# A hybrid attention block on one core: the indexer's keys projected in its queries' loop, first weights as two half loads, selection rounds spread, a gate moved ahead of the sparse values

## The chip, the cores and the metric

The kernel runs on one core of one Trainium2 chip. The metric is device time in microseconds (us), the median of several executions. Before the change it is 780.78 us, the median of three (780.55, 780.78, 782.25). The engines are TensorE (PE, matmuls; PEld is its weight load), VectorE (DVE), ScalarE (ACT), GpSimd (POOL) and SyncE (SP), which here only issues DMAs. Each runs its own list of instructions in a fixed order and waits at semaphores for the others.

## What is computed

One block of an encoder over 512 positions and 1024 channels, in float32:

```python
proj = x @ w_in[layer]
q_a, k_a, v_a, q_i, k_i, w_i, q_s, k_s, v_s, g_a, g_b = jnp.split(proj, IN_OFFSETS, axis=-1)
y_a = dsa_sequence(...)     # sparse attention
y_s = sb_sequence(...)      # stick-breaking attention
merged = sigmoid(g_a + b) * (y_a @ w_branch_dsa) + sigmoid(g_b + b) * (y_s @ w_branch_sb)
x = layer_norm(ALPHA * x + merged @ w_out, ...)
u, g = jnp.split(x @ w_ffn_in, 2, axis=-1)
h = gelu(causal_dwconv(u, conv_w, conv_b)) * g
x = layer_norm(ALPHA * x + h @ w_ffn_out, ...)
```

The sparse branch chooses its keys with an "indexer": from queries q_i (8 heads of 64), one shared set of keys k_i (64 wide) and 8 weights w_i per position it computes a score per pair, the sum over heads of w_i * relu(q_i . k_i), and keeps the 128 best keys of each query. Then it is ordinary attention over those, with a relative bias, 8 heads. The stick-breaking branch has 8 heads too; its weights are products of sigmoids along the keys, which a running product (a scan) gives.

## The kernel before

**Numbers.** A float32 matrix is used as a sum of a rounded high half and a low half (`whi`/`wlo`, `xh`/`xl`). Each product is three matmuls: high by high, high by low, low by high. ScalarE makes the high half (L94, L261), VectorE or, for the weights named in `POOL_LO`, GpSimd the low half by a subtraction (L96, L262).

**Weights.** `Stream` (L52) holds the list `order` of all weight pieces, up to 512 KB each. A `get` loads three pieces ahead (L85) into raw buffers and splits three ahead (L86) into a ring of three pairs `whi`, `wlo`. There are three raw buffers (`rawp`, L128); before the change the eight pieces of the indexer's query weights have other raw buffers, the four tiles of tag "q" (L245). All loads are issued by SP, and up to the 13th piece an explicit order holds them in the order of the program (L66).

**PSUM.** Two pools of four banks each, `psA` and `psB` (`pa` and `pb` in the code). A tile takes a bank until all that reads it is done.

**Who orders the work.** The program is written as one list. A planner then simulates it with its own costs and gives each engine its order: of the instructions that are ready and have a buffer, it takes the one that stands first in the program. `tc.issue_after` adds an order on one engine by hand.

**Start (L175 to L280).** Nine matmuls on zeros (`WARM`) run first. Then a loop over the eight chunks k of 128 channels loads and splits the chunk of x and the chunk `qi{k}` of the indexer's query weights and adds 12 matmuls of 384 columns to the four banks `qps` (queries 128 to 511; the first 128 need no selection). In the first two rounds of the loop, four steps (`next(values)`) of the stick-breaking values are done too, with half pieces `vs00` and `vs01`; their four sums are in `psB`.

**Indexer (L313 to L376).** `idx_queries` (L313) empties the four `qps` banks into the halves `qi`. Behind 12 matmuls of filling, `idx_keys` (L324) projects keys and weights w_i (24 matmuls of 512 columns, 72 rows out) and empties them. Then two small matmuls build the bias line (L551). `idx_scores` computes 24 dots (three query blocks j, eight heads; two matmuls each in a `psA` bank), each with a relu on ScalarE (L353) and an accumulation on VectorE (L358). `select` (L360) takes 16 rounds for each block j: a round finds the 8 largest of a row (L367) and replaces them (L368), so 48 rounds in all. `select_some(n)` puts n of them at that place of the program. 16 stand between the dots, and the others behind the scans of the first seven stick-breaking heads, by `ROUNDS = 3, 3, 4, 5, 5, 6, 6`.

**Filling.** The list `FILL` (L32) names the projections that TensorE does between the parts of the heads, in order: `vs`, `qs`, `ks` are the stick-breaking values, queries and keys, `va`, `qa`, `ka` the sparse ones, `gb`, `ga` the gates, `bs` the branch's output. `fill(n)` (L528) emits steps of three matmuls until n are out. `proj_t` (L196) makes one 128-row block in a `psA` bank; `proj_v` (L208) makes values in four banks at once, over eight chunks. They are emptied by ScalarE and VectorE (L231 and L232 for values, L305 and L306 for queries, L295 to L297 for keys, ScalarE alone for gates).

**Heads (L576 to L593).** Sixteen heads in turn, eight stick-breaking, eight sparse. In each: the next head's logits, `fill(15)`, transposes of this head's weights (L389), the next head's scans on VectorE (L445), the rounds, `fill(15)`, the weighing (L405), `fill(15)`. The first sparse head needs all selections done (L569).

**Behind the heads.** The merge, the output projection, the first norm. Each block of 128 positions is normed on VectorE (L656 last) and transposed on TensorE by `turn` (L699), whose result is split by ScalarE (L707) and VectorE (L708) into `x1h`, `x1l`. The feed-forward part (L719) takes its first three pieces in two halves of the positions, `t_lo` for all three, then `turn` for the last block, then `t_hi` for all three. The rest is not touched.

Of the kernel before, what the change touches and what calls it, by code (L numbers as in the profile page):

```python
# [31 lines left out]
FILL = ("vs qs0 ks0 qs1 ks1 qs2 ks2 gb0 gb1 qs3 ks3 gb2 gb3 qa0 ka0 gb4 qa1 ka1 va gb5 bs0 bs1 qa2 ka2 gb6 gb7 bs2 bs3 "  # L32
        "qa3 ka3 ga0 ga1 ga2 ga3 ga4 ga5").split()
GAP = 15
ROUNDS = 3, 3, 4, 5, 5, 6, 6
# [16 lines left out]
class Stream:  # L52


    def __init__(self, tc, raw, ring, pieces, ahead_load, ahead_split, place=None, lo_on_pool=()):
        self.tc, self.nc, self.raw, self.ring, self.pieces, self.last = tc, tc.nc, raw, ring, pieces, None
        self.place = {} if place is None else place
        self.raw_place = {}
# [22 lines left out]

    def _advance(self, upto):
# [3 lines left out]
        while self.ns < min(n, upto + self.asp, self.nl):  # L86
# [7 lines left out]
            nc.scalar.activation(hi[:, :w], t[:, :w], AF.Copy)  # L94
# [14 lines left out]
def tile_block(ctx: ExitStack, tc: tile.TileContext, xT, xN, w_qi, w_ki, w_t, w_v, w_br, w_o, w_fi, w_fo,  # L109
# [33 lines left out]
    order = [(f"qi{k}", w_qi[k]) for k in range(KC)]  # L143
    for kk in (1, 0):
        order.insert(kk + 1, (f"vs0{kk}", w_v[0, 0][:, kk * 512:kk * 512 + 512]))
    order.append(("vs1", w_v[0, 1]))

    def pieces(t):
        if t == "ki":
            return [(t, w_ki)]  # L150
        if t in ("vs", "va"):
            return [(f"{t}{g}", w_v[int(t == "va"), g]) for g in range(2 * (t == "vs"), 4)]
# [4 lines left out]
    for t in ["ki"] + FILL:  # L157
# [13 lines left out]
    place = {}  # L171
# [24 lines left out]
    def proj_t(key, M=128, bank=pa):  # L196

        wh, wl = st.get(key)
        ps = bank(f"{key}_ps")
        for k in range(KC):  # L200
            c = slice(k * M, k * M + M)
            nc.tensor.matmul(ps[:M], wh[:, c], xh[k], start=(k == 0), stop=False)  # L202
            nc.tensor.matmul(ps[:M], wh[:, c], xl[k], start=False, stop=False)  # L203
            nc.tensor.matmul(ps[:M], wl[:, c], xh[k], start=False, stop=(k == KC - 1))  # L204
            yield 3
        return ps

    def proj_v(which, name):  # L208

        pss = [(pb if which == "vs" else pa)(f"{name}_ps{i}") for i in range(NB)]  # L210
        for g in range(4):
            halves = which == "vs" and g == 0
            if not halves:
                wh, wl = st.get(f"{which}{g}")
            for kk in range(2):
                k = 2 * g + kk
                c = slice(kk * 512, kk * 512 + 512)
                if halves:
                    wh, wl = st.get(f"{which}{g}{kk}")
                    c = slice(0, 512)  # L220
                for i in range(NB):
                    r = slice(i * 128, i * 128 + 128)
                    nc.tensor.matmul(pss[i], xh[k][:, r], wh[:, c], start=(k == 0), stop=False)
                    nc.tensor.matmul(pss[i], xh[k][:, r], wl[:, c], start=False, stop=False)
                    nc.tensor.matmul(pss[i], xl[k][:, r], wh[:, c], start=False, stop=(k == KC - 1))
                    yield 3
        vt = []
        for i in range(NB):
            v = bp.tile([128, H, 2, 64], F32R, tag="v", bufs=4, name=f"{name}{i}")
            src = pss[i].rearrange("p (h d) -> p h d", h=H)  # L230
            nc.scalar.activation(v[:, :, 0, :], src, AF.Copy)  # L231
            nc.vector.tensor_sub(v[:, :, 1, :], src, r32(v[:, :, 0, :]))  # L232
            vt.append(v)
# [688 lines left out]
```

## Time and profile before

| what | value |
|---|---|
| median of three executions | 780.78 us |
| the profiled execution's own time | 781.24 us |
| its span, first to last instruction | 779.5 us |
| TensorE busy | 767.4 us (98%) |
| VectorE busy | 473.9 us (61%) |
| ScalarE busy | 331.1 us (42%) |
| GpSimd busy | 117.6 us (15%) |
| moved by DMA | 84.01 MB |
| granted TensorE clock, mean | 0.999 |

How to read the lines: a time, a duration, the engine, the line of the kernel, the operation, the tiles written and read, the shapes, a count, and in brackets how long the engine had been idle and what ended it. Groups have count, busy time in us, mean ns of one, and idle time before. Matmuls are pipelined: the profile's duration of one reaches past the start of the next. TensorE's busy share hides short waits, so the distance from one start to the next is of more use.

### The profile page before, as it was taken

Reading aid. Unit: us, or ns where it says so; the run is one execution under the profiler, and the core shown is the slowest. Engines: PE = TensorE matmul, PEld = TensorE weight load, DVE = VectorE, ACT = ScalarE, POOL = GpSimd, SP = SyncE. Lnnn points to the kernel's source line nnn. Section 1 sums busy time; section 2 is a strip of 40 time slices with the busy share of each in tenths; the row PEclk is TensorE's granted clock in tenths of the full one; section 3 lists DMA queues with packets and bytes.
Section 4 is the critical chain, followed back from the end, with each engine's and each line's share of the span. In section 5 each row is a group of like instructions: output and inputs, shape, how many; then the busy total and the mean of one; then the engine's idle time right before and its main releaser. Section 6 shows DMA issues by size and latency. Waiting matters only on the chain.

```text
span 779.5 us, 9704 instructions
## 1 busy us (share of the span) xinstructions
PE 767.4 (98%) x3696; PEld 643.8 (83%) x3696; DVE 473.9 (61%) x782; ACT 331.1 (42%) x518; POOL 117.6 (15%) x123
## 2 busy tenths in 40 slices
PE   9999999999999999999999999999999999999996
PEld 7878888887788888888889888888888888888885
DVE  5579776899887665477744545435354543536345
ACT  5474665564555837745102433323323332332300
POOL 1012464446634210000001000000000000000002
PEclk9999999999999999999999999999999999999999
DMA  7445413222323232127502333222222222322302
GB/s 260 144 152 175 134 56 109 93 71 81 108 94 124 84 131 78 61 99 259 209 0 79 114 106 104 85 82 109 107 98 93 108 82 82 112 104 80 138 27 82
DMA packets 26591, 84.01 MB, mean 108 GB/s; under 512 B 3816, under 2 KB 4200, under 8 KB 26544
## 3 DMA queue, kind: packets, MB, share of 16 engines
q1 hardware_dynamic: 22320, 72.87, 26.2%
q10 hardware_dynamic: 2576, 6.29, 3.0%
q0 software_dynamic: 1648, 4.22, 1.6%
q8 instruction: 29, 0.48, 0.3%
q14 instruction: 18, 0.15, 0.1%
HBM read 77.06 MB, written 4.21 MB: 104 GB/s over the span
## 4 chain that ended last, share of the span: by engine, by line
PE 91%; DVE 7%; issue 1%; ACT 1%; POOL 1%; POOLq 0%; DVEq 0%; ACTq 0%
PE u_ps L724 5%; PE d_ps L752 5%; PE d_ps L753 5%; PE d_ps L754 5%; PE u_ps L725 5%; PE g_ps L724 5%; PE g_ps L723 5%; PE g_ps L725 5%; PE u_ps L723 5%; PE av_ps L405 2%; PE ga_ps L203 2%; PE ga_ps L202 2%; PE ga_ps L204 2%; PE o_ps L683 2%; PE o_ps L682 2%; PE o_ps L684 2%
## 5 line engine op out<-in xcount | busy, mean ns | idle before, releaser
L94 ACT ACTIVATE whi<-raw 128x1024 fp32r<-128x1024 f32 (+1 forms) x114 | 119.6, 1049 | 225.3 <-PE d_ps L754 84.9
L96 DVE TENSOR_TENSOR wlo<-raw,whi 128x1024 fp32r<-128x1024 f32 (+1 forms) x95 | 115.2, 1213 | 161.8 <-ACT whi L94 155.0
L723 PE MATMUL u_ps<-x1h,whi 128*128 128x512 f32 (+1 forms) x192 | 71.4, 372 | 0.2 <-ACT x1h L707 0.2
L724 PE MATMUL u_ps<-x1l,whi 128*128 128x512 f32 (+1 forms) x192 | 71.4, 372 | 0.1
L725 PE MATMUL u_ps<-x1h,wlo 128*128 128x512 f32 (+1 forms) x192 | 71.3, 371 | 0.0
L724 PE MATMUL g_ps<-x1l,whi 128*128 128x512 f32 (+1 forms) x184 | 69.9, 380 | 0.0
L723 PE MATMUL g_ps<-x1h,whi 128*128 128x512 f32 (+1 forms) x184 | 69.9, 380 | 0.0
L725 PE MATMUL g_ps<-x1h,wlo 128*128 128x512 f32 (+1 forms) x184 | 69.9, 380 | 0.0
L752 PE MATMUL d_ps<-whi,hh 128*128 128x512 f32 (+1 forms) x178 | 65.5, 368 | 0.0
L753 PE MATMUL d_ps<-wlo,hh 128*128 128x512 f32 (+1 forms) x178 | 65.4, 368 | 0.0
L754 PE MATMUL d_ps<-whi,hl 128*128 128x512 f32 (+1 forms) x178 | 61.4, 368 | 0.0
L96 POOL TENSOR_TENSOR wlo<-raw,whi 128x1024 fp32r<-128x1024 f32 x19 | 45.8, 2412 | 34.8 <-ACT whi L94 34.8
L731 POOL MEMSET u<- 128x2 f32 x22 | 2.2, 101 | 268.7 <-DVE c L736 260.8
L723 PEld LDWEIGHTS u_ps<-x1h,whi 128*128 128x128 f32 x192 | 36.2, 188 | 6.7 <-ACT x1h L707 0.5
L724 PEld LDWEIGHTS u_ps<-x1l,whi 128*128 128x128 f32 x192 | 36.2, 188 | 6.5 <-DVE x1l L708 0.3
L725 PEld LDWEIGHTS u_ps<-x1h,wlo 128*128 128x128 f32 x192 | 36.2, 188 | 6.3
L725 PEld LDWEIGHTS g_ps<-x1h,wlo 128*128 128x128 f32 x184 | 34.6, 188 | 6.6
L723 PEld LDWEIGHTS g_ps<-x1h,whi 128*128 128x128 f32 x184 | 34.6, 188 | 6.5
L724 PEld LDWEIGHTS g_ps<-x1l,whi 128*128 128x128 f32 x184 | 34.6, 188 | 6.4
L737 ACT ACTIVATE c<-c,cwt 128x512 f32<-128x512 f32 x22 | 15.9, 723 | 55.6 <-DVE c L736 55.6
L394 DVE TENSOR_TENSOR ptl<-tr_ps,pth 128x512 fp32r<-128x512 f32 (+1 forms) x48 | 27.9, 594 | 18.2 <-ACT pth L393 17.6
L753 PEld LDWEIGHTS d_ps<-wlo,hh 128*128 128x128 f32 x178 | 33.6, 189 | 5.6
(463 smaller groups left out, 1775.3 us busy)
## 6 DMA issues: line engine op xcount, KB each, us to landing
raw<-in_w_fi_dram SPq DMA_DIRECT2D x44, 512.0 KB, 3.2
raw<-in_w_t_dram SPq DMA_DIRECT2D x32, 512.0 KB, 3.3
raw<-in_w_fo_dram SPq DMA_DIRECT2D x22, 512.0 KB, 3.2
raw<-in_w_br_dram SPq DMA_DIRECT2D x8, 512.0 KB, 3.1
raw<-in_w_o_dram SPq DMA_DIRECT2D x8, 512.0 KB, 3.8
raw<-in_w_v_dram SPq DMA_DIRECT2D x7, 512.0 KB, 4.2
xr<-in_xT_dram SPq DMA_DIRECT2D x8, 256.0 KB, 4.8
raw_qi<-in_w_qi_dram SPq DMA_DIRECT2D x8, 256.0 KB, 4.9
```

The costliest lines, as they stand in the source:

```text
L94: nc.scalar.activation(hi[:, :w], t[:, :w], AF.Copy)
L96: eng.tensor_sub(lo[:, :w], t[:, :w], r32(hi[:, :w]))
L202: nc.tensor.matmul(ps[:M], wh[:, c], xh[k], start=(k == 0), stop=False)
L203: nc.tensor.matmul(ps[:M], wh[:, c], xl[k], start=False, stop=False)
L394: lows = nc.vector.tensor_sub(tl[:, :width], ps[:, :width], r32(th[:, :width]))
L723: nc.tensor.matmul(ps[:, c], wh[:, kc], x1h[:, k, c], start=(k == 0), stop=False)
L724: nc.tensor.matmul(ps[:, c], wh[:, kc], x1l[:, k, c], start=False, stop=False)
L725: nc.tensor.matmul(ps[:, c], wl[:, kc], x1h[:, k, c], start=False, stop=(k == KC - 1))
L737: nc.scalar.activation(c, c, AF.Gelu_apprx_tanh, bias=cwt[:, f, 3:4])
L752: nc.tensor.matmul(ps, hh[f][:, r], wh[:, c], start=start, stop=False)
L753: nc.tensor.matmul(ps, hh[f][:, r], wl[:, c], start=False, stop=False)
L754: nc.tensor.matmul(ps, hl[f][:, r], wh[:, c], start=False, stop=stop)
```

## The change

- **Keys in the queries' loop.** The indexer's key weights `ki` become the fourth piece of the stream and are split into two tiles of tag "q". From the second round of the loop on, the three key matmuls of the chunk follow the twelve of the queries (in the second round those of both chunks), in a bank of `psB`. `idx_keys` then only empties that bank. The bias line is built straight behind the loop.
- **Values.** The stick-breaking values are no longer begun in the loop. They start as the first filling, in the four `psA` banks, with whole pieces. In the last of the four pieces (g = 3) the steps of both kinds of values are sorted by block, so that one block is finished after the other.
- **Banks.** The dots and the transposed weights w_i use `psB`, not `psA`. The 12 matmuls of filling ahead of `idx_keys` go.
- **First weights.** `qi0` is loaded as two halves of 256 columns, `qi00` and `qi01`. The high half of the first is made by VectorE, those of all others by ScalarE as before; the first chunk's `xl` is ordered behind that copy. The query weights use the three raw buffers of `rawp` like all others.
- **Rounds.** `ROUNDS` goes. One round follows each scan, and `fill(15, 2)` places one more behind every second step of filling; two such fills a head make five rounds a head for the first seven.
- **FILL.** `gb5` stands before `va`, not behind it.
- **Feed-forward.** `turn` for the last block stands ahead of the third `t_lo` piece, not behind it.

The diff, without the functions that only move:

```diff
-FILL = ("vs ... qa1 ka1 va gb5 bs0 bs1 qa2 ka2 gb6 gb7 bs2 bs3 "
+FILL = ("vs ... qa1 ka1 gb5 va bs0 bs1 qa2 ka2 gb6 gb7 bs2 bs3 "
...
-ROUNDS = 3, 3, 4, 5, 5, 6, 6
...
-            if key in self.raw_place:
-                t = self.raw_place[key](key)
-            else:
-                t = self.raw.tile([128, 1024], F32, tag="raw", name=f"raw_{self.nl}")
+            t = self.raw.tile([128, 1024], F32, tag="raw", name=f"raw_{self.nl}")
...
-            nc.scalar.activation(hi[:, :w], t[:, :w], AF.Copy)
+            if self.ns:
+                nc.scalar.activation(hi[:, :w], t[:, :w], AF.Copy)
+            else:
+                self.first = nc.vector.tensor_copy(hi[:, :w], t[:, :w]).ins
...
-    order = [(f"qi{k}", w_qi[k]) for k in range(KC)]
-    for kk in (1, 0):
-        order.insert(kk + 1, (f"vs0{kk}", w_v[0, 0][:, kk * 512:kk * 512 + 512]))
-    order.append(("vs1", w_v[0, 1]))
+    order = [(f"qi0{i}", w_qi[0][:, i * 256:i * 256 + 256]) for i in range(2)]
+    order += [(f"qi{k}", w_qi[k]) for k in range(1, KC)]
+    order.insert(3, ("ki", w_ki))
...
+    place = {"ki": lambda key: [bp.tile([128, 1024], F32R, tag="q", bufs=4, name=key + h) for h in "hl"]}
...
+    kps = pb("ki_ps")
...
     for k in range(3):
         load_x(k)
-        st.load((2, 4, 5)[k])
+        st.load((2, 3, 5)[k])
     for k in range(KC):
...
         nc.scalar.activation(h, xr, AF.Copy)
-        nc.vector.tensor_sub(l, xr, r32(h))
+        if k == 0:
+            ws = [st.get("qi00"), st.get("qi01")]
+        with tc.issue_after(st.first):
+            nc.vector.tensor_sub(l, xr, r32(h))
...
+        if k == 1:
+            kw = st.get("ki")
+        for kk in () if k == 0 else (0, 1) if k == 1 else (k,):
+            c = slice(kk * 72, kk * 72 + 72)
+            nc.tensor.matmul(kps[:72], kw[0][:, c], xh[kk], start=(kk == 0), stop=False)
+            nc.tensor.matmul(kps[:72], kw[0][:, c], xl[kk], start=False, stop=False)
+            nc.tensor.matmul(kps[:72], kw[1][:, c], xh[kk], start=False, stop=(kk == KC - 1))
...
-        if k < 2:
-            for _ in range(NB):
-                next(values)
...
-        pss = [(pb if which == "vs" else pa)(f"{name}_ps{i}") for i in range(NB)]
+        pss = [pa(f"{name}_ps{i}") for i in range(NB)]
...
+            steps = [(kk, i) for kk in range(2) for i in range(NB)]
+            for kk, i in sorted(steps, key=lambda t: t[1]) if g == 3 else steps:
...
     def idx_keys():
-        ps = whole(proj_t("ki", M=72, bank=pa))
+        ps = kps
...
-        ps = pa("wi_ps")
+        ps = pb("wi_ps")
...
-                ps = pa("dot_ps")
+                ps = pb("dot_ps")
...
-    def fill(n):
+    def fill(n, every=0):
+        step = 0
         while n > 0:
             c = next(fillers, None)
             if c is None:
                 return
             n -= c
+            step += 1
+            if every and step % every == 0:
+                select_some(1)
...
     idx_queries()
-    fill(12)
     idx_keys()
...
             with tc.issue_after(scan):
-                select_some(ROUNDS[i])
-        fill(GAP)
+                select_some(1)
+            fill(GAP, 2)
+        else:
+            fill(GAP)
...
-        fill(GAP)
+        fill(GAP, 2 if i < H - 1 else 0)
...
     for w, ps in zip(w0, ps0):
+        if ps is ps0[2]:
+            turn(NB - 1)
         ffn_in(w, ps, t_lo)
-    turn(NB - 1)
     for w, ps in zip(w0, ps0):
         ffn_in(w, ps, t_hi)
```

More of the change, by code (lines that the diff above doesn't have):

```diff
@@ L31 @@
 TAKEN = -3.3e38
[L32 removed]
+FILL = ("vs qs0 ks0 qs1 ks1 qs2 ks2 gb0 gb1 qs3 ks3 gb2 gb3 qa0 ka0 gb4 qa1 ka1 gb5 va bs0 bs1 qa2 ka2 gb6 gb7 bs2 bs3 "
         "qa3 ka3 ga0 ga1 ga2 ga3 ga4 ga5").split()
 GAP = 15
[L35 removed]
 WARM = 9
@@ L193, in tile_block @@
     cwt = cst.tile([128, FC, 4], F32, name="cwt")
[L196 to L208, printed above, removed]
-        pss = [(pb if which == "vs" else pa)(f"{name}_ps{i}") for i in range(NB)]
[L211 to L233, printed above, removed]
-        return vt
     late = slice(NSEL, S)
@@ L240, in tile_block @@
     qps = [pa(f"qi_ps{n}") for n in range(4)]
-    values = proj_v("vs", "vs")
+    kps = pb("ki_ps")
     ohf = bp.tile([64, NREL], F32, tag="beta", bufs=2, name="ohf")
     rbf = padded(bp, [32, H], name="rbf")
-    for k in range(KC):
-        st.raw_place[f"qi{k}"] = lambda key: r32(bp.tile([128, 2, 512], F32R, tag="q", bufs=4, name=f"raw_{key}")[:, 0])
     xrs = {}
@@ L276, in tile_block, with proj_t @@
             st.queue(cwt.rearrange("p a b -> p (a b)"), cw)
-        if k < 2:
-            for _ in range(NB):
-                next(values)
+    oh = bp.tile([64, NREL], F32R, tag="beta", bufs=2, name="oh")
+    rb = edge.tile([64, H], F32R, name="rb")
+    nc.gpsimd.tensor_copy(oh, ohf)
+    nc.vector.tensor_copy(rb[0:32], rbf)
+    nc.vector.tensor_sub(rb[32:64], rbf, r32(rb[0:32]))
+    line = bp.tile([H, NREL], F32, tag="beta", bufs=2, name="line")
+    for a, b in ((0, 512), (512, NREL)):
+        ps = pb("line_ps")
+        nc.tensor.matmul(ps[:H, :b - a], rb, oh[:, a:b], start=True, stop=True)
+        nc.scalar.activation(line[:, a:b], ps[:H, :b - a], AF.Copy, scale=-1.0)
+    s_line = nc.dram_tensor("s_line", (H, NREL), F32, kind="Internal").ap()
+    s_win = nc.dram_tensor("s_win", (H, 128, 512), F32, kind="Internal").ap()
+    nc.gpsimd.dma_start(s_line, line)
+    nc.gpsimd.dma_start(s_win, bass.AP(tensor=s_line.tensor, offset=s_line.offset + 127,
+                                       ap=[[NREL, H], [-1, 128], [1, 512]]))
+    def proj_t(key):
+        wh, wl = st.get(key)
+        ps = pa(f"{key}_ps")
+        for k in range(KC):
+            c = slice(k * 128, k * 128 + 128)
+            nc.tensor.matmul(ps, wh[:, c], xh[k], start=(k == 0), stop=False)
+            nc.tensor.matmul(ps, wh[:, c], xl[k], start=False, stop=False)
+            nc.tensor.matmul(ps, wl[:, c], xh[k], start=False, stop=(k == KC - 1))
+            yield 3
+        return ps
     def whole(gen):
@@ L308, in stack_dup, with proj_v @@
         return a, b
+    def proj_v(which, name):
+        pss = [pa(f"{name}_ps{i}") for i in range(NB)]
+        for g in range(4):
+            wh, wl = st.get(f"{which}{g}")
+            steps = [(kk, i) for kk in range(2) for i in range(NB)]
+            for kk, i in sorted(steps, key=lambda t: t[1]) if g == 3 else steps:
+                k = 2 * g + kk
+                c = slice(kk * 512, kk * 512 + 512)
+                r = slice(i * 128, i * 128 + 128)
+                nc.tensor.matmul(pss[i], xh[k][:, r], wh[:, c], start=(k == 0), stop=False)
+                nc.tensor.matmul(pss[i], xh[k][:, r], wl[:, c], start=False, stop=False)
+                nc.tensor.matmul(pss[i], xl[k][:, r], wh[:, c], start=False, stop=(k == KC - 1))
+                yield 3
+        vt = []
+        for i in range(NB):
+            v = bp.tile([128, H, 2, 64], F32R, tag="v", bufs=4, name=f"{name}{i}")
+            src = pss[i].rearrange("p (h d) -> p h d", h=H)
+            nc.scalar.activation(v[:, :, 0, :], src, AF.Copy)
+            nc.vector.tensor_sub(v[:, :, 1, :], src, r32(v[:, :, 0, :]))
+            vt.append(v)
+        return vt
     qi, index = [], {}
@@ L504, in filler @@
         if kind in ("vs", "va"):
-            vals[kind[1]] = yield from (values if kind == "vs" else proj_v(kind, kind))
+            vals[kind[1]] = yield from proj_v(kind, kind)
         elif kind == "bs":
```

29 lines of the change are left out of this document (6 added, 23 removed).

## The prediction

> **What bounds the kernel now.** The page came first: its span and its line of busy times.
>
> ```profile
> span 779.5 us, 9704 instructions
> ...
> PE 767.4 (98%) x3696; PEld 643.8 (83%) x3696; DVE 473.9 (61%) x782; ACT 331.1 (42%) x518; POOL 117.6 (15%) x123
> ```
>
> TensorE (PE) is busy for all but 12 us of the span. The change leaves the number and the sizes of the matmuls as they are, so it can win only what TensorE loses by waiting, and it can lose by new waits. The view of who waited for whom, kept to TensorE, lists every wait:
>
> ```profile
> PE idle_ps L179 <- DVE idle L176: 1.2, 1, 1.2
> PE gb_ps L202 <- DVE va L232: 1.1, 1, 1.1
> PE dot_ps L350 <- ACT relu L353: 1.0, 1, 1.0
> PE va_ps L223 <- DVE ka1b L297: 0.9, 1, 0.9
> PE u_ps L723 <- ACT x1h L707: 0.2, 1, 0.2
> ```
>
> Below the launch there are four. The timeline of TensorE gives their places and true sizes, since matmuls overlap (a 512-column one is shown 0.39 us long, yet the next starts 0.22 to 0.23 us later):
>
> ```profile
> 52.41 0.28 PE L351 MATMUL dot_ps<-kil,qi3b 128*128 128x256 f32 x1
> 53.70 0.44 PE L350 MATMUL dot_ps<-kih,qi0a 128*128 128x384 f32 x1 [1.01 <-ACT relu L353]
> ...
> 188.24 0.39 PE L225 MATMUL va_ps<-whi,xl 128*128 128x512 f32 x1
> 188.46 0.39 PE L223 MATMUL va_ps<-whi,xh 128*128 128x512 f32 x1
> 189.79 0.47 PE L223 MATMUL va_ps<-whi,xh 128*128 128x512 f32 x1 [0.94 <-DVE ka1b L297]
> ...
> 211.17 0.50 PE L202 MATMUL gb_ps<-xh,whi 128*128 128x512 f32 x1 [1.07 <-DVE va L232]
> ```
>
> From start to start the wait at 189.79 costs 189.79 - 188.46 - 0.23 = 1.10 us. That at 53.70 costs 53.70 - 52.41 - 0.12 = 1.17 us (0.12 us is the step of 256 columns, shown below). That at 211.17 is 1.07 us idle plus some 0.16 us of lost overlap (0.39 - 0.23), about 1.2 us. All three are TensorE waiting for a psA bank that ScalarE or VectorE has not emptied yet. Why they are late is in the busy time by stretch (columns: stretch, its length, then PE, PEld, DVE, ACT, POOL busy):
>
> ```profile
> 28.00:48.00 20.00, 20.00 (x91) 14.90 (x90) 10.48 (x15) 8.92 (x15) 0.78 (x1) 1.00 0.34 120
> 48.00:80.00 32.00, 30.99 (x148) 25.74 (x147) 29.76 (x71) 19.39 (x38) 8.59 (x9) 1.00 0.52 164
> 80.00:150.00 70.00, 70.00 (x356) 59.29 (x355) 52.95 (x106) 43.76 (x80) 36.96 (x22) 1.00 0.30 98
> 150.00:206.00 56.00, 55.06 (x275) 46.19 (x274) 52.92 (x104) 29.76 (x55) 27.00 (x18) 1.00 0.28 90
> ```
>
> VectorE is half idle from 28 to 48 us (10.48 of 20), full from 48 to 80 (29.76 of 32), slack by 17 us from 80 to 150, and full again from 150 to 206 (52.92 of 56). The selection rounds run through all of it:
>
> ```profile
> L367 DVE MAX8 m<-score x48: 402/560/696, 58.2 to 198.8; 128x8 f32<-128x256 f32 x16, 128x8 f32<-128x384 f32 x16, 128x8 f32<-128x512 f32 x16
> ```
>
> **The change part by part.** *Start: two half loads, the first split by VectorE.*
>
> ```profile
> 0.73 0.37 SPq L67 DMA_DIRECT2D xr<-in_xT_dram  x1
> ...
> 1.16 0.42 SPq L67 DMA_DIRECT2D raw_qi<-in_w_qi_dram  x1
> ...
> 1.18 4.02 PE L179 MATMUL idle_ps<-idle 128*128 128x512 bf16 x9 [1.18 <-DVE idle L176]
> ...
> 3.23 0.63 ACT L261 ACTIVATE xh<-xr 128x512 fp32r<-128x512 f32 x1 [1.01 <-DMA xr<-in_xT_dram]
> ...
> 4.39 0.63 ACT L94 ACTIVATE whi<-raw_qi 128x512 fp32r<-128x512 f32 x1 [0.53 <-DMA raw_qi<-in_w_qi_dram]
> ...
> 5.06 0.69 DVE L96 TENSOR_TENSOR wlo<-raw_qi,whi 128x512 fp32r<-128x512 f32 x1 [0.47 <-ACT whi L94]
> 5.08 1.26 PE L268 MATMUL qi_ps<-xh,whi 128*128 128x384 f32 x4
> ```
>
> The first real matmul waits for its high half, 4.39 + 0.63 = 5.02 us. A load of half the size and a copy beside ScalarE's make that earlier by up to 1 us. But the nine warm-up matmuls stay and fill TensorE from 1.18 to 5.20, the last handing over near 5.0. The gain is between 0 and 0.08 us; I take 0.
>
> *Start: loads through three buffers.* The query weights lose four raw buffers of their own ("q") and share the three of rawp with the key weights. SP issues in order, so each x chunk behind a waiting weight load is late too, and ScalarE's xh after it.
>
> ```profile
> raw_qi<-in_w_qi_dram SPq DMA_DIRECT2D x8, 256.0 KB, 4.9
> ```
>
> One buffer is held for 4.9 us of landing plus 0.63 and 0.69 of split, 6.2 us; three of them pass a piece every 2.1 us. TensorE needs a chunk every 12 x 0.17 + 3 x 0.23 = 2.7 us (0.17 is three quarters of 0.23), so the steady state holds. The first round may not: the third query chunk waits for the second half's buffer, free near 5.7, and at 4.9 + 0.63 is there at 11.2, where TensorE comes at 5.08 + 2.1 + 2.1 + 1.4 = 10.7; the next may be 0.3 late as well. With the 2.5 us of the first load (0.73 to 3.23) nothing is late. Bounds 0 and 1.0; fewer loads are in flight than before, so I take 0.2.
>
> *Keys in the loop.* The 24 key matmuls take the place of 24 value matmuls at the same width: nothing in TensorE's time. The price is a new hand-over: the stick-breaking values now need the psA banks that hold the queries.
>
> ```profile
> L350 PE MATMUL dot_ps<-kih,qi0a x3: 279/432/441, 47.6 to 56.6; 128*128 128x256 f32 x1, 128*128 128x384 f32 x1, 128*128 128x512 f32 x1
> ```
> ```profile
> L270 PE MATMUL qi_ps<-xh,wlo x32: 331/334/346, 7.6 to 27.6; 128*128 128x384 f32 x32
> ```
> ```profile
> 28.15 0.56 DVE L321 TENSOR_TENSOR qi0b<-qi_ps,qi0b 64x384 fp32r<-64x384 f32 x1
> ...
> 32.85 0.56 DVE L321 TENSOR_TENSOR qi3b<-qi_ps,qi3b 64x384 fp32r<-64x384 f32 x1
> ```
>
> With the keys' sums ready at 27.6 and ScalarE and VectorE some 5 us busy with the queries first, the dots, and after them VectorE's scores and rounds, start near 33 rather than 47.6, some 14 us earlier, in the half-empty stretch. The banks come free between 28.7 and 33.4. In strict order TensorE would lose 33.4 - 27.6 - 3 x 0.68 = 3.8 us. The other bound is 0: the last key matmuls cover 0.7 us, and the first bank can take the steps of the next chunks. Before, the order written by the planner also ran ready work ahead, so I take 0.4.
>
> *Values to the first queries.* qs0 needs a bank that VectorE must empty of values, and these subtractions stand behind scores and rounds.
>
> ```profile
> 58.52 0.44 PE L202 MATMUL qs_ps<-xh,whi 128*128 128x512 f32 x1
> ```
>
> TensorE comes there at about the same time, 58.52 less the wait of 1.2 plus four dots still to run (8 x 0.23): 59. VectorE's work of 28 to 80 us, 10.48 + 29.76 = 40.2 us, would last until 68.2 without a hole. So the bounds are 0 and 9 us. In the new code the last group of values is finished block by block, so the first bank can be emptied 2 us and more before; and VectorE puts other ready work between the two halves of a round, as the sum of a head's values here, straight behind the round's search:
>
> ```profile
> 159.52 0.69 DVE L367 MAX8 m<-score 128x8 f32<-128x512 f32 x1
> 160.24 0.68 DVE L411 TENSOR_TENSOR yst<-av_ps,avt 64x512 f32<-64x512 f32 x1
> ```
>
> I take 0.4. The old wait at 53.70 (1.17) goes, because dots use psB and values remain to run beside them.
>
> *Rounds spread.* Before, 3, 3, 4, 5, 5, 6, 6 rounds follow the heads; after, five each until the 32 are done, so the last two heads carry 5 + 2, not 12.
>
> ```profile
> L367 DVE MAX8 m<-score 128x8 f32<-128x512 f32 x16 | 10.9, 684 | 0.2
> L368 DVE MATCH_REPLACE8 score<-m,score 128x512 f32<-128x512 f32 x16 | 10.8, 675 | 0.0
> ...
> L368 DVE MATCH_VALUE_LOAD score<-m,score 128x8 f32 x48 | 4.2, 88 | 1.2
> ```
>
> Five rounds of 0.684 + 0.675 + 0.088 = 1.45 us are 7.2 us less in the stretch 150 to 206, where VectorE is 1.1 to 1.2 us late twice. They fit into the 17 us of slack before. If that cover were gone, the two waits would stay.
>
> *The gate between ka1 and va.* It puts 24 matmuls (5.4 us) between the emptying of ka1's bank and the values that need it; the wait at 189.79 has two reasons to go. Behind va now comes bs0, which needs va's first bank; sorted, that block ends 18 matmuls (4.1 us) before the last, so the wait at 211.17 should not return there. Together 1.10 + 1.2.
>
> *The last turn in the feed-forward part.*
>
> ```profile
> 412.31 1.41 DVE L656 SCALAR_TENSOR_TENSOR r<-r,rstd,ln 128x512 f32<-128x512 f32 x2
> ...
> 417.53 0.28 PE L725 MATMUL u_ps<-x1h,wlo 128*128 128x256 f32 x1
> 417.65 1.04 PE L705 MATMUL xt_ps<-ident,r 128*128 128x128 f32 x8
> ...
> 419.66 0.38 PE L724 MATMUL u_ps<-x1l,whi 128*128 128x256 f32 x1
> ```
>
> After the transposes three matmuls run, then TensorE waits for x1l until 419.66: at least 419.66 - 417.65 - 1.04 - 3 x 0.12 = 0.6, with overlap 0.7 us. The change puts 24 matmuls (2.9 us) behind the transposes, more than the 2.0 us they need, and the block they turn is ready at 413.7, before 414.8. Gain 0.7.
>
> **Sum.** The profiled execution took 781.24 us (779.5 span, 1.7 around it), 0.46 above the median 780.78. 1.17 + 1.10 + 1.2 + 0.7 = 4.2 off, 0.2 + 0.4 + 0.4 = 1.0 on: 778.0, and less 0.46, **777.6**.
>
> **Rivals.** *The waits move.* For: VectorE stays full from the dots on, and the wait for relu came from ScalarE's queue, which is not shorter. Against: 14 us earlier start. With the wait of 1.17 back, one of 1.2 kept, new ones of 1.5: 777.6 + 1.17 + 1.2 + 0.5 = 780.5, no change.
>
> *Slower: the hand-over from values to qs0.* If the planner puts the four subtractions behind the rounds, TensorE has nothing else to run at 59 us. It decides from where the wait eats the whole gain and 0.2%: 0.4 + (782.3 - 777.6) = 5.1 us. Midway between that and the bound of 9, 7 us, gives 777.6 + 6.6 = 784.2. Against: before, TensorE lost nothing from 59 to 80 beside an equally full VectorE. The granted clock is 1.00 in all four stretches above. The Trainium skill (TensorE: Matmul & The Clock Gate, Part 1) has the clock halved after about 3.4 us without work and restored after as long of work; by that rule, which no wait of this trace is long enough to show, this rival would cost about 1.7 us more, 785.9 by estimate.
>
> *No new wait at all:* 781.24 - 4.2 - 0.46 = 776.6.
>
> **Chances.** Forecast 0.53, waits move 0.23, slower 0.14, no new wait 0.10. A difference of 0.2% (1.6 us) is about what a measurement here tells from none: 779.2 to 782.3 is "same". Faster: 0.53 + 0.10 and little of the rest, 0.64; same 0.21; slower 0.15. The forecast's own range is 776.6 to 779.2. The whole reaches from 775.9 (0.7 below, should small waits go too) to 782.2, which leaves out the slower rival and little more.
>
> **What would show it.** Right: the first dot near 33 us rather than 47.6; the last round starting before 190 rather than at 198.8; no wait on ka1b or va; L724 following the third L723 by 0.12 us. Wrong: TensorE waiting for qi subtractions after 27.6 by more than 1 us, for values before qs0, or for whi between 7 and 14 us.

## The result, and the profile after

| kernel | median us | lowest to highest | executions |
|---|---|---|---|
| before | 780.85 | 780.55 to 782.25 | 4 |
| after | 791.15 | 790.67 to 793.45 | 4 |

The change makes the kernel slower: ratio 1.0134, 95% interval 1.0111 to 1.0157, 10.3 us. The forecast was 777.6, range 775.9 to 782.2. The profiled execution of the kernel after took 791.4 us, 10.2 us more than that of before. Its page, with its own line numbers (all lines below are those of the kernel that is named):

```profile
span 789.6 us, 9716 instructions
...
PE 770.3 (98%) x3696; PEld 645.3 (82%) x3696; DVE 479.9 (61%) x783; ACT 331.5 (42%) x517; POOL 115.5 (15%) x123
```

The 3696 matmuls are the same. What TensorE waited for, in the kernel after (us in total, times, longest):

```profile
PE z_ps L446 <- DVE ks0a L287: 2.8, 1, 2.8
PE av_ps L420 <- DVE ptl L409: 2.3, 1, 2.3
PE qs_ps L268 <- DVE vs L321: 2.1, 1, 2.1
PE va_ps L312 <- ACT gb L531: 1.9, 1, 1.9
PE va_ps L312 <- DVE ka1b L288: 1.5, 1, 1.5
...
```

(Left out is the one at the launch, 1.2 as before.) The waits for `relu` (1.0) and for x1h (0.2) of before are gone, as forecast, and so is that of a gate's bank for `va` (1.1). That for ka1b stays and is longer, and four new ones of 1.9 to 2.8 us stand there. By stretch (columns as in the prediction):

```profile
28.00:48.00 20.00, 20.00 (x97) 16.12 (x96) 12.51 (x21) 10.24 (x22) 1.90 (x2) 1.00 0.49 165
48.00:80.00 32.00, 29.92 (x136) 24.78 (x135) 25.16 (x58) 15.86 (x28) 3.59 (x6) 1.00 0.36 113
```

VectorE does a little more ahead of 48 us than before (12.51 instead of 10.48), but from 48 to 80 it does 25.16 us of work instead of 29.76: it stands still where it was to be full. Its timeline shows where, and GpSimd's shows why:

```profile
44.78 2.25 DVE L373 SCALAR_TENSOR_TENSOR score<-relu,wi,score 128x256 f32<-128x256 f32 x4 [0.55 <-ACT relu L368]
54.60 0.43 DVE L382 MAX8 m<-score 128x8 f32<-128x256 f32 x1 [7.57 <-POOL score L379]
```
```profile
35.83 1.12 POOL L258 DMA_DIRECT2D s_win<-s_line  x1 [1.62 <-DMA s_line<-line]
53.71 0.14 POOL L469 MEMSET win<- 64x64 f32 x1 [16.75 <-DMA win<-s_win]
...
54.42 0.14 POOL L379 MEMSET score<- 64x64 f32 x1
```

The first score block is summed at 44.78 + 2.25 = 47.0. Before its first round a corner of it is filled by a memset on GpSimd (L379, 0.14 us). In the kernel after, the bias line is built right behind the queries' loop, so the planner knows the windows early and puts the memsets of the first two windows (L469) ahead of the score's. But the windows are a transfer of a transfer, started at 35.83 and there at 53.7. GpSimd waits 16.75 us at its head, and VectorE, whose order has the round next, waits 7.57 us behind it, until 54.60. The two waits of TensorE nearest behind that are those for VectorE's `vs` (its product starts at 58.19) and `ks0a` (83.41).

The other loss lies between 187 and 215. The timelines of ScalarE, VectorE, GpSimd and TensorE in turn, and the stretch behind:

```profile
199.41 1.28 ACT L531 ACT_TABLE_LOAD   x1
200.70 0.69 ACT L531 ACTIVATE gb<-gb_ps,bgt 128x512 f32<-128x512 f32 x1
201.41 1.28 ACT L490 ACT_TABLE_LOAD   x1
```
```profile
204.37 5.19 DVE L496 TENSOR_SCALAR lg<-lg,rs 128x128 f32<-128x128 f32 x4
209.48 1.61 DVE L409 TENSOR_TENSOR ptl<-tr_ps,pth 128x512 fp32r<-128x512 f32 x3
```
```profile
203.82 3.01 POOL L473 TENSOR_TENSOR bm<-win,score 128x256 f32<-128x256 f32 x3
206.79 2.48 POOL L94 TENSOR_TENSOR wlo<-raw,whi 128x1024 fp32r<-128x1024 f32 x1
```
```profile
210.21 0.51 PE L420 MATMUL av_ps<-ptl,vs 128*128 128x512 f32 x1 [2.29 <-DVE ptl L409]
```
```profile
210.00:215.00 5.00, 4.79 (x18) 4.18 (x19) 3.12 (x10) 2.32 (x6) 0.00 (x0) 0.66 0.42 129
```

The gate that was moved has its Sigmoid among the first sparse head's Exp, with a table load of 1.28 us on either side. The head's four scalings (L496) end late and take 5.19 us; the same four took 1.28 us in the kernel before:

```profile
204.88 1.28 DVE L481 TENSOR_SCALAR lg<-lg,rs 128x128 f32<-128x128 f32 x4
```

Behind them TensorE waits 2.29 us, and then the granted clock is 0.66 on the mean from 210 to 215.

### The profile page after: what moved, and what is told of

It reads as the page before. It is cut to its first block, busy times and chain, and to the rows that moved or that the text cites. A ratio compares the mean times of both kernels' runs of the same rounds, so it can differ in the third digit from the quotient of the medians.

```text
span 789.6 us, 9716 instructions
## 1 busy us (share of the span) xinstructions
PE 770.3 (98%) x3696; PEld 645.3 (82%) x3696; DVE 479.9 (61%) x783; ACT 331.5 (42%) x517; POOL 115.5 (15%) x123
## 4 chain that ended last, share of the span: by engine, by line
PE 72%; DVE 1%; POOL 0%; POOLq 0%; issue 0%
PE d_ps L756 5%; PE d_ps L757 5%; PE d_ps L758 5%; PE u_ps L728 5%; PE u_ps L727 5%; PE g_ps L728 5%; PE u_ps L729 5%; PE g_ps L727 5%; PE g_ps L729 5%; PE ga_ps L270 2%; PE ga_ps L269 2%; PE ga_ps L268 2%; PE o_ps L686 2%; PE o_ps L688 2%; PE o_ps L687 2%; PE av_ps L420 1%
## 5 line engine op out<-in xcount | busy, mean ns | idle before, releaser
L94 DVE TENSOR_TENSOR wlo<-raw,whi 128x1024 fp32r<-128x1024 f32 (+2 forms) x102 | 119.6, 1173 | 162.9 <-ACT whi L90 162.6
L90 ACT ACTIVATE whi<-raw 128x1024 fp32r<-128x1024 f32 (+2 forms) x120 | 123.8, 1032 | 216.9 <-PE d_ps L758 90.5
L756 PEld LDWEIGHTS d_ps<-whi,hh 128*128 128x128 f32 x178 | 33.5, 188 | 5.6
```

Source lines behind the costliest of these rows:

```text
L94: eng.tensor_sub(lo[:, :w], t[:, :w], r32(hi[:, :w]))
L756: nc.tensor.matmul(ps, hh[f][:, r], wh[:, c], start=start, stop=False)
```

## The experiments

The theory after the traces: the loss has three parts, (1) the score memset behind the windows, (2) the gate's Sigmoid, (3) the rounds' spread or what goes with it. Each is undone in the kernel after, alone and with the others, and the parts are done alone in the kernel before. Ratios are to the kernel before, with 95% intervals.

| kernel | median us | ratio |
|---|---|---|
| after, score memset on VectorE | 784.90 | 1.0052 (1.0037 to 1.0067) |
| after, bias line back | 785.08 | 1.0059 (1.0044 to 1.0074) |
| after, gate back | 790.47 | 1.0117 (1.0102 to 1.0132) |
| memset, gate back | 783.04 | 1.0026 (1.0016 to 1.0036) |
| memset, rounds back | 780.84 | 1.0000 (0.9991 to 1.0009) |
| memset, gate and rounds back | 778.78 | 0.9973 (0.9963 to 0.9983) |
| memset, gate, rounds back, whole load | 778.18 | 0.9970 (0.9957 to 0.9982) |
| before, bias line early | 781.61 | 1.0008 (0.9999 to 1.0018) |
| before, gate swapped | 783.22 | 1.0032 (1.0020 to 1.0043) |
| before, rounds spread | 784.55 | 1.0048 (1.0033 to 1.0063) |
| before, last turn moved | 780.18 | 0.9989 (0.9979 to 0.9998) |

### The score memset

```diff
-                nc.gpsimd.memset(sc[0:64, N - 64:N], INVALID)
+                nc.vector.memset(sc[0:64, N - 64:N], INVALID)
```

> The kernel after, with one edit: the memset of each score tile (the one that fills its corner with INVALID) is issued on VectorE instead of GpSimd; the bias line, its two transfers and the window memsets stay where the change put them. Theory A (the first selection round is held by GpSimd's queue: the score memset stands behind two window memsets that wait 16.75 us for the transfer of the windows, until 53.71): the first MAX8 starts near 48 instead of 54.6, VectorE is some 6 us ahead, the TensorE waits at 58.19 (2.24) and 83.41 (2.96) go, and the time falls by 4 to 5.5 us, to 785.5 to 787. Rival B (VectorE is late by its sum of work up to there, wherever the first round starts): the two waits stay within 1 us of what they were and the time stays at 790.5 to 791.5.

784.90, 6.25 us less than the kernel after; theory A, and 0.6 us beyond its range. A row of VectorE's timeline and TensorE's waits in this kernel:

```profile
47.33 0.43 DVE L382 MAX8 m<-score 128x8 f32<-128x256 f32 x1
```
```profile
PE av_ps L420 <- DVE ptl L409: 2.3, 1, 2.3
PE va_ps L312 <- ACT gb L531: 1.9, 1, 1.9
PE va_ps L312 <- DVE ka1b L288: 1.5, 1, 1.5
...
```

Both waits ahead of 90 us are gone, with GpSimd's queue and the transfers as they were. The same from the other side, the change's own part undone (the block `oh` to `s_win` moved; `...` stands for the rest of it, and its removal from the old place is left out):

```diff
     idx_queries()
     idx_keys()
+    oh = bp.tile([64, NREL], F32R, tag="beta", bufs=2, name="oh")
+    ...
     for j in idx_scores():
```

> The kernel after with one of its parts undone: the block of the bias line goes back behind the indexer's keys, as in the kernel before. GpSimd's order then has the first score memset ahead of the two window memsets, the second score memset behind them. Theory A (the loss of 5 to 6 us ahead of 90 is the first score memset behind the windows' transfer, and nothing else of the change): the first MAX8 starts near 47 to 49, the waits at 58.19 and 83.41 are gone or under 1 us in all, and the time is 784.9 to 787, as with the memset on VectorE. Rival B (the second memset, now behind a later transfer, stops the second block's rounds instead): the first MAX8 is early, but VectorE stands idle at the second block and the time is 787 to 792.

785.08, theory A: the first score memset runs at 48.44 on GpSimd, ahead of the window memsets (59.37), and the first MAX8 at 48.62. The second score memset, behind them at 62.43, was itself waiting for VectorE's score, so the windows hold nothing up there. And the early line put into the kernel before:

> The kernel before, with one edit: the block that builds the bias line and starts the two transfers of the line and of the windows is moved ahead of the twelve products of values, thus ahead of the indexer's keys. Theory A (GpSimd's queue holds the first round where the windows' memsets stand ahead of the score memset and wait for the transfer): the first MAX8 is late against the dots, by some us, TensorE waits for VectorE later on, and the time rises by 2 to 6 us, to 783 to 787. Rival B (the early line is harmless by itself; the loss of the change comes from the keys' place and the rounds' spread): the time stays within 1 us of 780.85.

781.61, rival B. GpSimd in this kernel:

```profile
56.81 0.14 POOL L454 MEMSET win<- 64x64 f32 x1 [17.58 <-DMA win<-s_win]
...
59.19 0.14 POOL L364 MEMSET score<- 64x64 f32 x1 [1.58 <-DVE score L358]
```

The order is the bad one here too, and GpSimd waits even longer. But the dots are late in the kernel before, the score is not summed until 59, and the windows are there by then. So the cost is neither the early line's nor the early keys' alone: early keys bring the score to 47, the early line puts a wait until 53.7 ahead of it.

### The gate

```diff
-FILL = ("... qa1 ka1 gb5 va bs0 bs1 ...
+FILL = ("... qa1 ka1 va gb5 bs0 bs1 ...
```

> The kernel after, with the sixth gate put back behind the sparse values (list order ka1 va gb5 bs0, as before). Theory A (the gate's Sigmoid now stands in ScalarE's order among the first sparse head's Exp, between two table loads, and costs 2.04 us at 201.44 and part of the slow clock behind it): the wait on the gate goes, a wait for ka1b of 1 to 1.6 us comes back near 190 to 195, and the time falls by 1.5 to 4 us, to 787 to 789.6. Rival B (the stretch 187 to 215 is late because the rounds stand closer and VectorE is late, not because of the gate): the time stays within 1 us of 791.15.

790.47, 0.7 us less, which speaks for rival B. Its trace says that theory A's gain was there and lost elsewhere: the wait for the gate is gone and the one for `ptl` near 210 with it, but that for ka1b is 2.4 us, a new one of 1.3 us stands at 254, and behind the wait at 84 the clock is at 0.70 from 86 to 90, where the kernel after had 1.00. So the next kernels have the memset on VectorE, which takes that wait away:

> The kernel after with two edits: the score memset on VectorE, and the sixth gate back behind the sparse values. Measured so far: the first edit alone 784.9, the second alone 790.5. Theory A (a gate's Sigmoid among the first sparse head's Exp costs what the trace of the first edit shows between 189 and 208: waits of 1.65, 2.04 and 2.46 us and a stretch of slow clock): the wait for the gate and that of 2.46 us go, one wait for ka1b of 1 to 2.6 us stays, and the time is 781 to 783. Rival B (what the gate gives is lost again one head later, as the second edit alone showed with a new wait of 1.48 us at 254): 783.5 to 785.

783.04, 1.86 us less than with the memset alone: 0.04 us outside theory A's range and 0.5 outside rival B's. Rival B's wait is there too, 1.47 us at 246.92 from start to start. Its counterpart, which differs from the 778.78 us kernel by the gate's place alone (the diff above the other way round):

> The kernel after with the score memset on VectorE and the selection rounds dealt as in the kernel before (3, 3, 4, 5, 5, 6, 6); the gate stays ahead of the sparse values. It differs from the kernel of 778.78 us by the gate's place alone. Theory A (the gate by itself costs: its Sigmoid and two table loads of 1.28 us stand among the first sparse head's Exp, whatever the rounds do): 780.5 to 783. Rival B (the gate fills the wait for ka1b of 1.24 us, as the prediction had it, and cost time only beside the spread rounds): 777.5 to 779.

780.84, 2.06 us more, theory A. And the gate's part alone in the kernel before:

> The kernel before with the change's gate part alone: gb5 ahead of va in the list. The prediction priced it at 2.3 us gained (the waits of 1.10 at 189.79 and 1.23 at 211.17), that is 778.5. Theory A (the Sigmoid lands in ScalarE's order between Exp and Exp, with two table loads, and TensorE waits for the gate's place in the bank): no gain or a loss, 780.5 to 783. Rival B (the prediction's own): 778 to 779.6.

783.22, 2.55 us more; theory A, and just beyond its range. ScalarE and the waits in this kernel:

```profile
190.23 0.40 ACT L475 ACTIVATE lg<-lg,mn 128x128 f32<-128x128 f32 x1 [3.30 <-DVE mn L473]
...
192.73 1.28 ACT L516 ACT_TABLE_LOAD   x1
194.03 0.69 ACT L516 ACTIVATE gb<-gb_ps,bgt 128x512 f32<-128x512 f32 x1
...
195.22 1.28 ACT L475 ACT_TABLE_LOAD   x1
```
```profile
PE va_ps L223 <- ACT gb L516: 1.8, 1, 1.8
PE va_ps L223 <- DVE ka1b L297: 0.9, 1, 0.9
```

The gate was to cover the wait for ka1b. That wait (0.9) is as in the kernel before, and a second one, for the gate's own bank, is added: the bank is emptied at 194.03 + 0.69, behind a table load. The table load is the smaller part of that delay. The gate's last product starts at 186.28, but ScalarE's order has the first sparse head's Exp ahead of the Sigmoid, and ScalarE stands idle for 3.30 us, until 190.23, because that Exp waits for VectorE. Nor do the gate's products add cover for ka1b: the wait comes behind 24 of the gate and 7 of `va` here, and behind 31 of `va` in the kernel before. The gate holds one of the four `psA` banks itself, and the order is the planner's; why it comes to 31 both times is not shown.

Three pairs put the gate's place at 1.86 to 2.55 us; the fourth, with the score memset on GpSimd, gives 0.7. The trace of the swap alone accounts for less than its 2.55: its profiled execution, 782.45, is one of the fastest of its kernel, and its span is only 1.2 us longer than before.

### The rounds

```diff
+ROUNDS = 3, 3, 4, 5, 5, 6, 6
 ...
-                select_some(1)
-            fill(GAP, 2)
-        else:
-            fill(GAP)
+                select_some(ROUNDS[i])
+        fill(GAP)
 ...
-        fill(GAP, 2 if i < H - 1 else 0)
+        fill(GAP)
```

> As the run before it, and the selection rounds dealt as in the kernel before (3, 3, 4, 5, 5, 6, 6 behind each head instead of one every second step of the filling work). What is left of the change is the keys in the queries' loop, the half loads, the early bias line and the FFN's turn. Theory A (with the score memset out of GpSimd's queue the spread of the rounds is no longer what makes VectorE late): within 1 us of the run with the rounds spread. Rival B (spread rounds stand ahead of ka1's subtractions and cost the wait near 190): 1 to 2 us less than the run with the rounds spread, to below 781.

778.78, 4.26 us less than with the rounds spread: rival B's direction, at twice its price. This kernel is faster than the kernel before, and its list of TensorE's waits has two entries:

```profile
PE idle_ps L176 <- DVE idle L173: 1.2, 1, 1.2
PE va_ps L313 <- DVE ka1b L289: 1.1, 1, 1.1
```

The spread alone, in the kernel before (the diff the other way round):

> The kernel before with the rounds' part of the change alone: one selection round every second step of the filling work instead of 3, 3, 4, 5, 5, 6, 6 behind the heads. Theory A (the spread brings the last scan of sticks to where GpSimd is at a low half of a weight, so that it takes 5.12 us instead of 3.99 and ka1b comes 1.3 us later; and the four TENSOR_SCALAR of a sparse head meet GpSimd's work): the wait near 190 grows by about 1.3 us, a new one shows near 250, and the time rises by 2 to 4.3 us, to 783 to 785. Rival B (the spread is harmless as long as the dots are not early): within 1 us of 780.9.

784.55, 3.88 us more (beside 780.67, the kernel before measured with it), theory A in the time. In this kernel, the waits, TensorE's timeline near 190, the stretch there, and the timelines of VectorE and GpSimd:

```profile
PE va_ps L223 <- DVE ka1b L297: 2.4, 1, 2.4
PE av_ps L405 <- DVE ptl L394: 1.1, 1, 1.1
```
```profile
187.23 0.39 PE L224 MATMUL va_ps<-wlo,xh 128*128 128x512 f32 x1
190.02 0.52 PE L223 MATMUL va_ps<-whi,xh 128*128 128x512 f32 x1 [2.40 <-DVE ka1b L297]
190.34 0.63 PE L224 MATMUL va_ps<-wlo,xh 128*128 128x512 f32 x1
```
```profile
190.00:194.00 4.00, 3.98 (x11) 3.14 (x12) 3.58 (x10) 1.74 (x5) 2.37 (x4) 0.57 0.00 0
```
```profile
182.74 5.12 DVE L445 TENSOR_TENSOR_SCAN keep<-keep,first 128x128 f32<-128x128 f32 x4
189.18 0.69 DVE L297 TENSOR_TENSOR ka1b<-ka_ps,ka1b 64x512 fp32r<-64x512 f32 x1
237.50 2.48 DVE L417 TENSOR_TENSOR ya0l<-yat,ya0h 128x512 fp32r<-128x512 f32 x1 [0.75 <-ACT ya0h L416]
241.44 5.14 DVE L481 TENSOR_SCALAR lg<-lg,rs 128x128 f32<-128x128 f32 x4
```
```profile
182.74 2.62 POOL L96 TENSOR_TENSOR wlo<-raw,whi 128x1024 fp32r<-128x1024 f32 x1 [3.15 <-ACT whi L94]
237.04 2.39 POOL L96 TENSOR_TENSOR wlo<-raw,whi 128x1024 fp32r<-128x1024 f32 x1
243.52 2.46 POOL L96 TENSOR_TENSOR wlo<-raw,whi 128x1024 fp32r<-128x1024 f32 x1
```

The expectation had the scan right (5.12 us) and its consequence wrong. VectorE reaches the scan at 182.74 instead of 183.66, because fewer rounds stand ahead of it, and loses that 0.92 us and 0.2 more inside the scan, beside GpSimd's low half. ka1b starts at 189.18, only 0.23 us later than before (188.95). The wait at 190 grew by 1.46 us (1.10 to 2.56, from start to start) because TensorE came there 1.2 us sooner: from the first product of `va` to the wait, its order has 26 of them instead of 31 (5 x 0.23 = 1.15 us). The order is the planner's; that it did so because its costs gave VectorE the time that the scan then lost is only argued. Behind the wait the steps are 0.43 us instead of 0.23 until 193.7, at a clock of 0.57 (1.6 us more for 8 steps). The wait at 211 (1.2) is gone as forecast, and one at 247 is new (1.23). Together that is 1.46 + 1.6 - 1.2 + 1.23 = 3.1 us, the difference of the two profiled spans (782.6 and 779.5). Whether VectorE is late there for GpSimd's sake was put to a test of its own:

```diff
-POOL_LO += [f"va{g}" for g in range(4)]
+POOL_LO = [t for t in POOL_LO if t not in ("gb6", "gb7")] + [f"va{g}" for g in range(4)]
```

> The kernel before with the rounds spread, as measured at 784.55, and the low halves of two gate weights (gb6, gb7) taken from GpSimd to VectorE. In the trace of the spread alone these two run on GpSimd at 237.04 and 243.52; VectorE's subtraction at 237.50 took 2.48 us beside the first, the four TENSOR_SCALAR at 241.44 took 5.14 us up to the end of the second, and TensorE then waited 1.23 us at 247.25. Theory A (VectorE stands still while the GpSimd instruction beside it runs): the subtraction takes about 0.7, the four TENSOR_SCALAR no more than 3.5 us (the three sums of masks stay on GpSimd), the wait at 247 goes, and the time is 782.8 to 784 although VectorE has 2.4 us more to do. Rival B (VectorE is late there by its own work): the wait stays or grows, 784.5 to 786.

783.32 (ratio 1.0032, 1.0020 to 1.0044). The interval overlaps that of the spread alone, so a gain in time is not shown; what the timeline shows is theory A's mechanism:

```profile
238.88 0.69 DVE L417 TENSOR_TENSOR ya0l<-yat,ya0h 128x512 fp32r<-128x512 f32 x1
...
241.03 3.00 DVE L481 TENSOR_SCALAR lg<-lg,rs 128x128 f32<-128x128 f32 x4
```

2.48 became 0.69 and 5.14 became 3.00, and the wait at 247 is gone. The profiled execution is no shorter (span 782.6 in both): it has a wait of 1.43 us at 7.86 for a weight's high half, which the other has not. The same edit in the kernel after with the memset on VectorE, for other weights:

```diff
-POOL_LO += [f"va{g}" for g in range(4)]
+POOL_LO += ["va0"]
```

> The kernel after with the score memset on VectorE and three of the four low halves of the dense values' weights (va1, va2, va3) taken from GpSimd to VectorE. Theory A (a VectorE instruction that runs beside a GpSimd one ends only with it: the four TENSOR_SCALAR at 198.70 took 5.20 us instead of 1.28 while GpSimd had a sum of masks and a low half on hand, and the scan at 182.15 took 5.12): without the low halves on GpSimd the four TENSOR_SCALAR take under 3.5 us, the wait of 2.46 us at 204.5 shrinks by over 1 us, and the time falls by 1 to 2.5 us, to 782.4 to 783.9, although VectorE gets 3 times 1.2 us more work. Rival B (the slow instructions are slow for themselves, and the extra work makes VectorE later): the four still take about 5 us and the time is 784.9 to 787.

782.75 (1.0025, 1.0014 to 1.0035), theory A: 2.15 us less with some 3.7 us more for VectorE to do (three subtractions of 1.22 us where nothing holds them up), and the wait for `ptl` is gone from the list. Scan and scalings:

```profile
182.16 2.96 DVE L460 TENSOR_TENSOR_SCAN keep<-keep,first 128x128 f32<-128x128 f32 x4
199.18 1.76 DVE L496 TENSOR_SCALAR lg<-lg,rs 128x128 f32<-128x128 f32 x4
```

They were 5.12 and 5.20 us. But it is no general remedy; the same edit in the 778.78 us kernel:

> The fastest kernel so far (778.78 us: score memset on VectorE, gate back behind the values, rounds as before) with the low halves of va1, va2 and va3 on VectorE instead of GpSimd. Theory A (GpSimd's instructions that run beside VectorE's are what makes ka1b late, the last wait of over 1 us): the wait of 1.24 us at 189.2 shrinks to under 0.6 and the time is 777.8 to 778.6. Rival B (with twelve rounds behind the last two heads VectorE is full there, and 3.7 us more work make it later): 779 to 781.

781.44 (1.0010, 1.0001 to 1.0019), rival B, and somewhat beyond it. The wait for ka1b is gone, but two of 0.9 and 1.1 us stand near 210 with a clock of 0.66 from 210 to 215. That VectorE has no room there, with twelve rounds behind the last two heads, fits the trace (busy for 26 of the 28 us from 187 to 215) and is not shown beyond it. The profiled execution, 782.53, is the slowest of its ten and has two more waits, 0.4 us at 7.93 and 0.8 at 29.59, that are not rival B's.

### Half loads and the last turn

```diff
-    order = [(f"qi0{i}", w_qi[0][:, i * 256:i * 256 + 256]) for i in range(2)]
-    order += [(f"qi{k}", w_qi[k]) for k in range(1, KC)]
-    order.insert(3, ("ki", w_ki))
+    order = [(f"qi{k}", w_qi[k]) for k in range(KC)]
+    order.insert(2, ("ki", w_ki))
 ...
-            if self.ns:
-                nc.scalar.activation(hi[:, :w], t[:, :w], AF.Copy)
-            else:
-                self.first = nc.vector.tensor_copy(hi[:, :w], t[:, :w]).ins
+            nc.scalar.activation(hi[:, :w], t[:, :w], AF.Copy)
```

> As the first run of this call (score memset on VectorE, gate back), and the first weights as one whole load, split by ScalarE, as in the kernel before. Theory A (the half loads let the first product start at 4.64 instead of near 5, but the start is no gain: the products run with slow steps of 0.32 us until 6.6, and keys and queries end 0.58 us later than in the kernel before): the time changes by less than 0.4 us against the first run of this call. Rival B (the half loads bring 0.3 us or more): it is 0.3 to 1 us slower. Rival C (they cost): 0.3 to 0.6 us faster.

782.62 (1.0023, 1.0014 to 1.0032) beside the 783.04 of "memset, gate back": 0.42 us faster, just outside theory A and within rival C's range.

> The same fastest kernel with the first weights as one whole load, split by ScalarE, so that of the change only the keys' place, the early bias line and the last turn are left. Theory A (the half loads bring nothing, as in the other pair): within 0.4 us of 778.8. Rival B (they bring 0.4 us or more): 779.2 to 779.8.

778.18 beside 778.78: 0.2 us beyond theory A on the side that none had. Both pairs have the whole load 0.4 to 0.6 us ahead, which is rival C's size, and in both the intervals overlap: the half loads bring nothing, and whether they cost is not settled.

```diff
     for w, ps in zip(w0, ps0):
+        if ps is ps0[2]:
+            turn(NB - 1)
         ffn_in(w, ps, t_lo)
-    turn(NB - 1)
```

> The kernel before, with the change's last edit alone: the turn of the fourth block moved ahead of the third low half of the FFN's first products. The prediction priced it at 0.7 us gained: 780.85 goes to 780.1 (779.9 to 780.4). Rival: the wait only moves to the next product and the time stays within 0.2 us.

780.18 beside 780.87, 0.7 us, as priced, and the wait for x1h is gone from the list. The interval (0.2 to 1.6 us) only just leaves the rival out.

## Why the prediction was wrong, step by step

Undone one after the other, the parts lead from 791.15 to 778.78: 6.25 us for the memset, 1.86 for the gate, 4.26 for the rounds. As steps of one chain these add up by themselves. Undone or done beside other parts, the memset gave 6.1 to 7.4 us where the keys are early, the gate 0.7 to 2.55, the rounds 3.9 to 4.3: their order is safe, the split is not exact. The change without those three is priced by the prediction's own terms at 780.78 - 1.17 - 0.7 + 1.0 = 779.9. The measured 778.78 is 1.1 us less; in its trace the wait at 211 (1.2), which that price keeps, is gone even without spread and swap. So that part of the prediction held, a little too dear; three steps failed.

**"Keys in the loop": the step that was missing, 6.1 to 6.25 us.** The prediction took the dots for earlier, which they are, and followed them to TensorE and to VectorE. It did not follow the block that moved with them: it has no term for the early bias line, which so stood at nothing, without a reason. Building the bias line behind the loop moves two transfers on GpSimd's queue and, through the planner, two memsets that wait for them, ahead of the memset without which no round starts. The timeline of GpSimd in the kernel before had both, a wait of 10.42 us for the windows, harmless behind the first score memset:

```profile
57.78 0.14 POOL L364 MEMSET score<- 64x64 f32 x1 [6.28 <-DVE score L358]
68.34 0.15 POOL L454 MEMSET win<- 64x64 f32 x1 [10.42 <-DMA win<-s_win]
```

**"Values to the first queries": the place right, the cause another.** The slower rival was a wait there of 7 us, because the planner puts the subtractions behind the rounds. TensorE did wait there for `vs`, 2.1 us, where the prediction had 0.4. But the rounds had not filled VectorE; it had stood still. With the memset on VectorE the wait is gone from the list.

**"Rounds spread": wrong in sign.** Priced as what lets the waits at 189.79 and 211.17 go, it cost 3.88 us alone and 4.26 in the other kernel. VectorE had 0.92 us less ahead of the scan and gave it back in the scan, beside GpSimd; the prediction counted VectorE's busy time as work that can be taken off, and part of it is waiting that the records show as busy. In the trace of before, the scans of one head and of the next show it, and GpSimd beside the second:

```profile
168.35 2.96 DVE L445 TENSOR_TENSOR_SCAN keep<-keep,first 128x128 f32<-128x128 f32 x4
183.66 3.98 DVE L445 TENSOR_TENSOR_SCAN keep<-keep,first 128x128 f32<-128x128 f32 x4
```
```profile
182.40 2.41 POOL L96 TENSOR_TENSOR wlo<-raw,whi 128x1024 fp32r<-128x1024 f32 x1 [3.15 <-ACT whi L94]
```

The same four scans take 1.02 us longer where GpSimd is at a low half. The Trainium skill (SBUF — State Buffer, Who interferes with whom) has VectorE and GpSimd share a port pair as an exclusive lock: scalings can take it, and VectorE instructions with two inputs in SBUF contend for it with what GpSimd reads there. The runs agree: with the low halves beside them off GpSimd the scalings took 3.00 instead of 5.14 and 1.76 instead of 5.20 us, the subtraction 0.69 instead of 2.48, the scan 2.96 instead of 5.12. The rest of the loss, five products out of the wait's cover and a slow clock, was not in the prediction either.

**"The gate between ka1 and va": wrong in sign.** 24 matmuls do stand there now, but the wait for ka1b stayed (0.9 in the kernel before with the swap alone), and the gate's own bank was late, by the Sigmoid's place behind Exps that wait for VectorE and by its table load: up to 2.55 us lost instead of 2.3 won in both waits. The prediction counted the 24 matmuls as cover on top of the values' products, where they took the place of as many, and it left out the step's one instruction on ScalarE.

**The start.** The first real product starts at 4.64, as the nine matmuls hand over at 4.6 and not 5.0, and keys and queries nevertheless end 0.58 us later than before (28.34 instead of 27.76): no gain, as forecast. Loads through three buffers (0.2): the list of the kernel after has no wait for them, those of other runs up to 0.8 us. And the hand-over from queries to values (0.4, up to 3.8) cost nothing in the kernel after: the values follow the line's product at 28.72 without a gap. In one other run it cost 0.8. The first dot came at 38.18, not near 33: VectorE's last split of the keys ends at 35.07, with a weight split of 1.23 us and a wait of 0.66 for ScalarE among its work on queries and keys, and TensorE's order has ready values ahead of the dot until 38.18. **The last turn** (0.7) was right.

**The clock.** The prediction put the slow rival at 785.9 where the clock is lost as well, by the Trainium skill (TensorE: Matmul & The Clock Gate, Part 1), which halves it after some 3.4 us without work. Here it went after a wait of 2.40 us at 190, in the spread alone, and not after one of 2.8 us at 83 in the kernel after: the trace differs from the page, and a wait in this range costs now its own length, now 1.6 us more (8 steps at 0.43 instead of 0.23). Two kernels that differ only in their first weights show it best: "memset, gate back" and the same with the whole load (782.62) both wait 2.40 us for ka1b, until 189.57 and 189.49, with the same products around it. From 190 to 194 the clock is 0.62 in the first and 1.00 in the second. So up to some 1.6 us between two profiled executions can be the clock's alone.

## What to carry to other kernels

When a piece of work is moved earlier, list all that it issues, down to memsets of 0.14 us, and ask of each engine's queue what now stands behind an instruction that waits for a transfer. Before a gain is read off VectorE's busy time, compare the durations of equal instructions: those that were longer than their twins here ran beside GpSimd, and less work ahead of the scan only made it longer. An activation of another table, put among a head's Exp, cost two table loads here; ask also what stands ahead of it in ScalarE's order, because it holds its PSUM bank until it has run.

## What the runs showed of the hardware

A VectorE instruction can last as long as the GpSimd instruction beside it: a 128x512 subtraction took 2.48 us beside a low half on GpSimd and 0.69 without it. A wait of TensorE of 2.4 to 2.6 us can be followed by 3.4 us at half the clock (steps of 0.43 us instead of 0.23 from 190.3 to 193.7), while one of 2.8 us was not, and of two waits of 2.40 us one was and one was not: not only the length decides, and what else does was not tried. The transfer of the windows from DRAM to DRAM, started at 35.83, let the load behind it start only at 50.94, 15 us later; SyncE's queue stood 9.8 us for it.
